# A gated-parallel backbone layer: the gate's sum and the query and key transposes placed later in TensorE's order

## The chip, the cores and the metric

The kernel runs on one core of a Trainium2 chip. The metric is the device time of one execution in microseconds (us), and the figure that counts is the median of several executions. Engines are named as the profile names them: PE is TensorE's matmul side and PEld its weight loads, DVE is VectorE, ACT is ScalarE, POOL is GpSimd, SP is the engine that issues the DMA transfers.

## The reference

The layer takes 1024 latent tokens and 256 context tokens of width 1024. Cut to what bears on the change:

```python
mod_x = silu(c) @ w_ada + b_ada              # shift, scale and gate of width 1024 each
sh_x, sc_x, g_x = split(mod_x, 3)
pl = project(modulate(x, sh_x, sc_x), w_in)  # one input projection, split in eleven parts
pc = project(modulate(ctx, sh_c, sc_c), w_in)
...                                          # (A) gated linear attention, both directions
q1, q2, k1, k2, dv = diff_streams(pl[5], pl[6], pl[7], diff_q_norm, diff_k_norm)
                                             # per head: t * rsqrt(mean(t^2) + eps) * gain
q1, q2, k1, k2 = apply_rope(...)             # latent tokens only
o_diff = diff_attention(q1, q2, [ck1, k1], [ck2, k2], [cv, dv], lam)   # (B)
out_x = combine(...)                         # gates, two branch projections, one output projection
x = x + g_x * out_x
```

Two things in it are touched. The gate `g_x` is the last third of `mod_x`: a vector of 1024 numbers, each a sum over 1024 products, which the kernel wants on all 128 partitions. The queries and keys of branch (B) are normalised per group of 64, rotated, and then needed transposed, with the head's channels on the partitions.

## The kernel before

**Stages.** A start (to some 80 us) makes the modulation and the normalised inputs, transposed. Then the input projection streams its weights in column blocks of 512: keys and queries of branch (A), a gate part, three parts as a seven-product block scheme (`pairs`, about 215 to 485 us), and from about 480 us the list `late` of `phase_a`: keys of branch (B) in two column halves (`dk`, 10 token tiles each), a gate part (`gg`), queries of branch (B) in two halves (`dq`, 8 token tiles each), and one block of a merge gate. Alongside these late jobs the four heads of the gated linear attention run (`gla_head`). Differential attention follows (about 910 to 1440 us), with the rest of the projections as filler, and the output projection ends the kernel. Products are made from a high and a low part of each float32 operand, three matmuls for one.

**The order is planned when the program is written.** The four compute engines are scheduled by hand (`manual_schedule`), so every engine runs its instructions in the order in which they are emitted, and only semaphores make it wait. The order of emission comes from a discrete-event planner, the class `Driver`. The tasks are Python generators. What a task yields is the time at which it wants to go on. `Driver.now` is the planned time of TensorE; `Driver.op` adds a cost for each instruction to the planned time of its engine and notes when each tile will be ready (`ready`). `At(t)` lets a task go on up to 1 us ahead of `t` (`AHEAD`), `AtPE(t)` not before TensorE's planned time has reached `t`:

```python
def _at(self, at, prio, gen):
    t = at
    t = max(t, self.now) if isinstance(t, AtPE) else max(t - self.AHEAD, self.now)
```

`when(x)` gives the planned time at which tile x is ready as `At`, `whenpe(x)` the same as `AtPE`. While a task waits for its time, the planner emits whatever other task is due, those of the lowest `prio` first; the projection's stream of matmuls has `prio` 9 and takes what is left. DMA issues are emitted by the same tasks onto SP's queue, in the same order; a `store` goes out when its source is planned to be ready. Buffers are counted: `acq(tag)` makes a task wait until a buffer of that tag is free in the plan, `rel(tag, e)` frees it at the planned time `e`. The tags that matter here: `raw` (3 buffers for weights as loaded), `w` (18), `p` (5), `pl` (4), `mm` (3 banks for projection results), `tp` (2 banks for transposes).

**The gate's sum.** `job_gate` (line 745) works through the 1024 gate columns in two halves. For each half it loads `w_ada` in four pieces into `raw`, and VectorE multiplies each of eight row blocks by its conditioning column and adds it into `gb`. Then one matmul of `gb` with a matrix of ones (`self.ones`) sums over the partitions into a `tp` bank (the trace shows it as two matmul records of tp<-gb,ones). VectorE adds the bias, GpSimd halves the result into `gb`, and behind both halves `gb` is stored to `d_gb`. `to_gla`, which exchanges buffers before the gated linear attention, waits for that store; the values are used in the output projection.

**Queries and keys.** `post_qk` (line 1312) runs once for each of the 20 + 16 tiles of `dk` and `dq`. It takes two `p` buffers, squares the projection result on ScalarE (p<-mm), applies gain and rotation on VectorE, sums the squares per group, and lets GpSimd form the power -0.5 (sm<-sm,nhalf) and scale the tile (p<-p,sm). Then TensorE transposes the tile in four blocks of 128 into a `tp` bank (tp<-ident,p), the two `p` buffers are released, ScalarE and VectorE split the result into two `pl` buffers, and two stores write them to `d_kT` or `d_qT`.

In the trace all matmuls have line 335 and all transposes line 361, because they are issued by the helpers `mm` and `tr`; instructions of ACT, DVE and POOL have line 197. They are told apart by the tiles' names.

Of the kernel before, what the change touches and what calls it, by code (L numbers as in the profile page):

```python
# [228 lines left out]
class Hybrid:  # L229
# [515 lines left out]
    def job_gate(self):  # L745


        a = self.a
        yield from self.acq("gb")
        gb = self.t("gb", [P, 2, 512])  # L750
        for n in range(2):
            o = 2048 + n * 512
            for kk in range(NK // 2):
                yield from self.acq("raw")
                raw = self.t("raw", [P, 2, 512])
                self.dma(raw, a["w_ada"][0][kk * 256:(kk + 1) * 256, o:o + 512].rearrange("(k p) c -> p k c", p=P))
                yield self.d.when(raw)
                for j in range(2):
                    k = 2 * kk + j
                    c = self.col[:, k:k + 1]  # L760
                    if k == 0:
                        e = self.dve.tensor_scalar(gb[:, n], raw[:, j], c, None, ALU.mult)
                    else:
                        e = self.dve.scalar_tensor_tensor(gb[:, n], raw[:, j], c, gb[:, n], ALU.mult, ALU.add)
                    yield e
                self.rel("raw", e)
            yield from self.acq("p")
            bias = self.t("p", [P, 512])
            self.dma(bias, a["b_ada"][0:1, o:o + 512].to_broadcast([P, 512]))
            yield self.d.whenpe(gb)  # L770
            yield from self.acq("tp")
            pm = self.t("tp", [P, 512])
            e = self.mm(pm, self.ones, gb[:, n], True, True)
            yield e
            yield self.d.when(bias)
            e = self.dve.tensor_tensor(bias, pm, bias, ALU.add)
            self.rel("tp", e)
            yield e
            self.rel("p", self.pool.tensor_scalar(gb[:, n], bias, 0.5, 0.0, ALU.mult, ALU.add))
        self.store([(self.d_gb, gb)], ("gb", 1), ev=self.ev_gb)  # L780
# [531 lines left out]
    def post_qk(self, isk, c, i, pm):  # L1312

        nc = self.nc
        g8 = lambda ap: ap.unsqueeze(1).to_broadcast([P, 8, 64])
        pv = pm.rearrange("p (g e) -> p g e", e=64)
        if isk and (c, i) == (1, 9):
            self.rel("hc", self.d.now, 16)
        yield self.ev_rope[isk]
        yield from self.acq("p", 2)  # L1320
        sq = self.t("p", [P, 8, 64])
        self.act.activation(sq, pv, AF.Square)
        ss = self.t("sm", [P, 8])
        r = self.t("p", [P, 8, 64])
        if i >= 8:
            e = self.dve.tensor_tensor(r, pv, g8(self.gains[:, isk, 0]), ALU.mult)
        else:
            e = self.dve.tensor_tensor(r, pv, g8(self.rope[:, 0, i]), ALU.mult)
        yield self.d.when(sq)
        self.dve.tensor_reduce(ss, sq, AX.X, ALU.add)  # L1330
        if i < 8:
            rv = sq.rearrange("p g (a h e) -> p g a h e", a=2, h=2)
            xv = pv.rearrange("p g (a h e) -> p g a h e", a=2, h=2)
            sv = self.rope[:, 1, i].rearrange("p (a h e) -> p a h e", a=2, h=2)
            for hh in range(2):
                e = self.dve.tensor_tensor(rv[:, :, :, hh], xv[:, :, :, 1 - hh],
                                           sv[:, :, hh].unsqueeze(1).to_broadcast([P, 8, 2, 16]), ALU.mult)
            self.dve.tensor_tensor(r, r, sq, ALU.add)
            if (c, i) == (1, 7):
                self.rel("rope", self.d.when(r))  # L1340
        self.rel("mm", e)
        yield self.d.when(ss)
        self.pool.tensor_scalar(ss, ss, 1.0 / 64, EPS, ALU.mult, ALU.add)
        self.pool.tensor_tensor(ss, ss, self.nhalf, ALU.pow)
        yield self.d.when(r)
        e = self.pool.tensor_tensor(r, r, ss.unsqueeze(2).to_broadcast([P, 8, 64]), ALU.mult)
        yield AtPE(e)
        yield from self.acq("tp")
        yield from self.acq("pl", 2)
        pt = self.t("tp", [P, 4, P])  # L1350
        rf = r.rearrange("p g e -> p (g e)")
        for j in range(4):
            e = self.tr(pt[:, j], rf[:, j * P:(j + 1) * P])
        self.rel("p", e, 2)
        yield e
        hi = self.t("pl", [P, 4, P], F32R)
        lo = self.t("pl", [P, 4, P], F32R)
        e = yield from self.split(pt, hi, lo)
        self.rel("tp", e)
        o = self.tok(i) if isk else i * P  # L1360
        dst = [self.d_kT[j][c] if isk else self.d_qT[c][:, :, j] for j in range(2)]
        self.store([(dst[j][:, :, o:o + P].rearrange("h p t -> p h t"), x) for j, x in enumerate((hi, lo))],
                   ("pl", 2), ev=self.ev_st["dk" if isk else "dq", c, i])
# [1131 lines left out]
```

## Time and profile before

| | us |
|---|---|
| median of 3 executions | 1676.13 |
| lowest and highest | 1675.11, 1677.49 |
| the profiled execution | 1676.87 |
| its span, first to last instruction | 1675.2 |

Busy shares of the span: PE 98%, PEld 81%, DVE 70%, ACT 48%, POOL 36%. A window line gives a stretch of the span, its length, the busy time of each engine in it with the number of instructions, the granted TensorE clock as a part of full speed, the share of the DMA engines and the rate. A timeline line gives start, duration, engine, line and operation, with the tiles written and read, and in brackets the idle time of the engine before it and what ended that. The duration of a group of matmuls includes the tail of its last one, which overlaps the next group.

### The profile page before, as it was taken

What the parts mean: (1) busy time and instruction counts of PE and PEld (TensorE: products, weight loads), DVE (VectorE), ACT (ScalarE), POOL (GpSimd) and SP (SyncE); (2) the same over time, 40 slices, a digit from 0 to 9 for tenths busy, and PEclk for the clock granted to TensorE, in tenths of its full rate; (3) what the DMA queues carried; (4) which work ended last, traced back from release to release, by engine and by line L of the source; (5) the groups of instructions that cost most, each with busy time, mean ns of one, the idle gap of its engine ahead of it and who ended that gap; (6) DMA issues with size and microseconds to landing.
All of it is one profiled execution on the core that took longest, in us unless ns stands there. A gap on an engine that the chain in (4) does not pass through costs nothing.

```text
span 1675.2 us, 24268 instructions
## 1 busy us (share of the span) xinstructions
PE 1634.8 (98%) x8389; PEld 1354.1 (81%) x8389; DVE 1166.3 (70%) x2019; ACT 796.3 (48%) x1640; POOL 606.4 (36%) x649
## 2 busy tenths in 40 slices
PE   7999999999999999999999999999999999999999
PEld 3688788888788888888878887888888888888887
DVE  4797853455578697687762878877887787438594
ACT  4766423343434535455441666665666556413141
POOL 1500200000156575464540544546565565700000
PEclk9999999999999999999999999999999999999999
DMA  8557947677573675646466244334336743277422
GB/s 304 175 204 259 326 163 248 230 276 276 201 251 120 187 218 174 186 137 177 123 187 162 68 122 129 106 107 133 114 107 196 247 126 108 65 255 250 158 78 76
DMA packets 248971, 294.44 MB, mean 176 GB/s; under 512 B 20712, under 2 KB 169104, under 8 KB 248848
## 3 DMA queue, kind: packets, MB, share of 16 engines
q1 hardware_dynamic: 248848, 292.90, 55.4%
q8 instruction: 66, 1.08, 0.3%
q14 instruction: 57, 0.47, 0.1%
HBM read 199.51 MB, written 93.32 MB: 175 GB/s over the span
## 4 chain that ended last, share of the span: by engine, by line
PE 43%; DVE 7%; ACT 3%; issue 2%; POOL 1%; DMA 1%; SPq 0%; ACTq 0%; DVEq 0%; POOLq 0%
PE mc L335 11%; PE mm L335 7%; PE mb L335 7%; PE s L335 6%; PE b L335 5%; DVE sm L197 4%; PE b L361 3%; ACT e L197 2%; DVE e L197 2%; PE go L335 1%; POOL at L197 1%; PE mz L335 1%; PE gs L335 1%; PE tp L361 1%; PE gt L335 1%
## 5 line engine op out<-in xcount | busy, mean ns | idle before, releaser
L335 PE MATMUL mm<-w,h 128*128 128x512 f32 x1260 | 319.1, 402 | 0.6 <-DVE w L197 0.4
L335 PEld LDWEIGHTS mm<-w,h 128*128 128x128 f32 x1260 | 231.9, 189 | 47.9 <-issue 1.0
L197 DVE TENSOR_REDUCE sm<-s 128x1 f32<-128x1024 f32 (+1 forms) x192 | 194.1, 1038 | 44.5 <-PE s L335 38.8
L335 PE MATMUL mb<-h,wt 128*128 128x512 f32 x744 | 202.0, 404 | 0.8 <-ACT ft L197 0.5
L197 ACT ACTIVATE e<-s,sm 128x1280 f32<-128x1280 f32 x128 | 170.1, 1333 | 60.8 <-DVE sm L197 50.0
L197 POOL TENSOR_TENSOR at<-ac,at 128x512 fp32r<-128x512 f32 x128 | 191.2, 1493 | 10.7
L197 POOL TENSOR_SCALAR at<-ac 128x512 fp32r<-128x512 f32 x128 | 101.3, 791 | 251.4 <-ACT ac L197 153.7
L335 PE MATMUL s<-hk,aq 128*128 128x512 f32 (+1 forms) x768 | 179.5, 366 | 6.1 <-ACT e L197 4.2
L335 PEld LDWEIGHTS mb<-h,wt 128*128 128x128 f32 x744 | 130.9, 189 | 24.4 <-ACT ft L197 2.2
L335 PEld LDWEIGHTS s<-hk,aq 128*128 128x128 f32 x768 | 120.5, 189 | 27.2 <-ACT e L197 11.7
L335 PE MATMUL mm<-h,w 128*128 128x512 f32 x576 | 137.6, 394 | 2.2 <-DVE h L197 1.1
L335 PE MATMUL mc<-h,wt 128*128 128x512 f32 x600 | 137.7, 390 | 0.0
L335 PE MATMUL b<-at,vv 128*128 128x256 f32 x960 | 131.3, 285 | 0.5 <-POOL at L197 0.3
L335 PEld LDWEIGHTS mc<-h,wt 128*128 128x128 f32 x600 | 112.1, 188 | 23.1
L335 PEld LDWEIGHTS mm<-h,w 128*128 128x128 f32 x576 | 106.9, 188 | 26.2 <-DVE h L197 1.6
L335 PEld LDWEIGHTS b<-at,vv 128*128 128x128 f32 x960 | 123.3, 190 | 5.7 <-POOL at L197 0.9
L197 DVE TENSOR_TENSOR w<-raw,w 128x512 fp32r<-128x512 f32 x120 | 92.6, 790 | 32.1 <-ACT w L197 30.9
L197 ACT ACTIVATE ac<-b 128x512 f32<-128x512 f32 x120 | 71.1, 601 | 90.9 <-PE b L361 84.2
L197 POOL TENSOR_TENSOR sm<-sm,nhalf 128x2 f32<-128x2 f32 (+2 forms) x94 | 102.3, 1089 | 26.0 <-DVE sm L197 20.8
L197 DVE SCALAR_TENSOR_TENSOR e<-e,sm,e 128x1280 f32<-128x1280 f32 x64 | 110.4, 1725 | 1.0
L197 ACT ACTIVATE w<-raw 128x512 fp32r<-128x512 f32 x120 | 72.5, 629 | 70.8 <-DVE raw L197 22.8
L197 POOL TENSOR_TENSOR p<-p,gdif 128x512 f32<-128x512 f32 x12 | 16.2, 1359 | 242.6 <-DMA d_dv<-pl 194.6
(283 smaller groups left out, 2914.2 us busy)
## 6 DMA issues: line engine op xcount, KB each, us to landing
raw<-in_w_in SPq DMA_DIRECT2D x63, 512.0 KB, 4.5
g<-d_s SPq DMA_DIRECT2D x32, 640.0 KB, 5.0
aq<-d_qT SPq DMA_DIRECT2D x128, 128.0 KB, 3.1
d_dv<-pl SPq DMA_DIRECT2D x40, 256.0 KB, 2.1
gv<-d_v SPq DMA_DIRECT2D x40, 256.0 KB, 3.1
d_kT<-pl SPq DMA_DIRECT2D x40, 256.0 KB, 2.9
hk<-d_kT SPq DMA_DIRECT2D x32, 320.0 KB, 4.9
vv<-d_dv SPq DMA_DIRECT2D x16, 640.0 KB, 5.7
```

The source lines that it names most:

```text
L197: self.ins = f(out, *args, **kw).ins
L335: self.ins = self.nc.tensor.matmul(out, lhsT, rhs, start=start, stop=stop, skip_group_check=more).ins
L361: self.nc.tensor.transpose(out, src, self.ident[:n, :n])
```

## The change

Two lines are changed, both times at which a task asks the planner to go on.

```diff
@@ job_gate
-            yield self.d.whenpe(gb)
+            yield AtPE(self.d.when(gb) + 4)
             yield from self.acq("tp")
             pm = self.t("tp", [P, 512])
             e = self.mm(pm, self.ones, gb[:, n], True, True)
@@ post_qk
         e = self.pool.tensor_tensor(r, r, ss.unsqueeze(2).to_broadcast([P, 8, 64]), ALU.mult)
-        yield AtPE(e)
+        yield AtPE(e + 1.5)
         yield from self.acq("tp")
         yield from self.acq("pl", 2)
```

In `job_gate` the matmul with the ones is emitted when TensorE's planned time is 4 us past the planned end of `gb`, where it was emitted at that end; this happens once in each of the two halves. In `post_qk` the four transposes are emitted when TensorE's planned time is 1.5 us past the planned end of the tile's scaling on GpSimd; this happens 36 times. The instructions themselves, their number, shapes and operands stay as they are. Everything that a task emits behind these points moves with them, and the planner may place the instructions of all later tasks differently.

## The prediction

> **What bounds the kernel now.** I read the busy shares of the page first, then the mean granted clock, then TensorE's waits over the whole span (columns: in total, times, longest).
>
> ```profile
> span 1675.2 us, 24268 instructions
> PE 1634.8 (98%) x8389; PEld 1354.1 (81%) x8389; DVE 1166.3 (70%) x2019; ACT 796.3 (48%) x1640; POOL 606.4 (36%) x649
> ...
> core 0: 1675.2 us, clock 0.998
> ...
> PE tp L361 <- DVE p L197: 5.0, 1, 5.0
> PE s L335 <- ACT e L197: 4.2, 9, 1.2
> ...
> PE tp L335 <- DVE gb L197: 2.5, 1, 2.5
> ...
> PE tp L361 <- POOL p L197: 2.2, 1, 2.2
> ```
>
> TensorE is busy for 1634.8 of 1675.2 us. An edit that only moves instructions takes none of this work away; it can touch the 40.4 us of idle time and what follows from them. Two waits belong to the edited lines: the gate's sum (tp from gb and ones) waited once for VectorE, 2.5 us, and a transpose (tp from p) waited once for GpSimd, 2.2 us. How these stand in their stretches I took from the busy time by window (window, length, busy time and count of PE, PEld, DVE, ACT, POOL, granted clock, DMA share, GB/s) and from the grouped line of the transposes between 480 and 880 us:
>
> ```profile
> 480.00:880.00 400.00, 397.21 (x2021) 334.82 (x2020) 303.27 (x557) 190.55 (x510) 223.44 (x279) 1.00 0.59 175
> 915.00:1440.00 525.00, 510.41 (x3069) 434.64 (x3069) 420.22 (x788) 317.66 (x647) 293.68 (x266) 1.00 0.44 127
> L361 PE MATMUL tp<-ident,p 128*128 128x128 f32 x144 | 21.7, 273 | 2.2 <-POOL p L197 2.2
> ```
>
> The 144 are 36 query and key tiles with four transposes each, and one tile of the 36 waits. (The 5.0 us at the head of the list lies ahead of 480 us, in the constants.) TensorE is idle for 400.00 - 397.21 = 2.79 us there, nearly all of it this one wait. The timeline shows both stalls with their neighbours:
>
> ```profile
> 171.47 22.62 PE L335 MATMUL mm<-w,h 128*128 128x512 f32 x99
> 193.72 1.43 DVE L197 SCALAR_TENSOR_TENSOR gb<-raw,col,gb 128x512 f32<-128x512 f32 x1 [0.25 <-DMA raw<-in_w_ada]
> 195.81 0.74 DVE L197 SCALAR_TENSOR_TENSOR gb<-raw,col,gb 128x512 f32<-128x512 f32 x1
> 196.60 2.08 PE L335 MATMUL tp<-gb,ones 128*128 128x512 f32 x2 [2.50 <-DVE gb L197]
> ...
> 860.14 1.64 POOL L197 TENSOR_TENSOR sm<-sm,nhalf 128x8 f32<-128x8 f32 x1
> 861.56 0.94 PE L335 MATMUL mm<-h,w 128*128 128x512 f32 x3
> 862.46 1.22 POOL L197 TENSOR_SCALAR_AFFINE_SELECT gsc<-gsc 128x256 f32<-128x256 f32 x2 [0.68 <-ACT gsc L197]
> 863.65 1.04 POOL L197 TENSOR_TENSOR p<-p,sm 128x512 f32<-128x512 f32 x1
> 864.75 0.67 PE L361 MATMUL tp<-ident,p 128*128 128x128 f32 x4 [2.24 <-POOL p L197]
> 865.16 0.41 DVE L197 TENSOR_TENSOR gsc<-gsc 128x256 f32<-128x256 f32 x1
> 868.87 0.59 PE L335 MATMUL go<-gsf,gqe 128*128 128x256 f32 x2
> 869.30 0.59 PE L335 MATMUL go<-gsb,gqe 128*128 128x256 f32 x2
> 870.16 0.60 PE L361 MATMUL tp<-ident,p 128*128 128x128 f32 x4
> ```
>
> In the first stall TensorE stands from 194.10 to 196.60 until VectorE's last product into gb ends at 196.55; that chain waited for a load. In the second it stands from 862.51 to 864.75: GpSimd scales the tile only after its two masks on gsc, and ends at 864.69. Behind each stall the clock drops, which two windows show:
>
> ```profile
> 196.25:199.66 3.41, 3.06 (x5) 1.83 (x6) 3.31 (x5) 2.34 (x4) 1.70 (x1) 0.50 0.91 275
> 865.26:868.67 3.41, 3.41 (x11) 2.69 (x10) 1.01 (x2) 0.60 (x1) 2.77 (x3) 0.50 0.95 244
> ```
>
> Twice the granted clock is 0.50 for 3.41 us. A mean of 0.998 leaves 0.002 x 1675.2 / 0.50 = 6.7 us at half speed in the whole span, so these 6.82 us are practically all of it. TensorE works for 3.06 and 3.41 us in them at half rate and so loses 1.53 and 1.71 us. The stalls cost 2.50 + 1.53 = 4.03 and 2.24 + 1.71 = 3.95 us, 7.98 together.
>
> **The change, part by part.** It adds and removes no instruction and no byte. The program writes its order against a planned clock; the change lets the gate's sum enter TensorE's order 4 planned us behind gb (two times), and each tile's four transposes 1.5 us behind the scaling (36 times). With 22.62 / 99 = 0.2285 us for a matmul in the stream, this is room for about 17 and 6 matmuls ahead of the moved ones, where the planner has them.
>
> Gate. The lateness was 2.50 us, the room is 4, so the stall goes and its half clock with it: -4.03 us. The bounds are -4.03, and 0 if the loads come later by as much as the sum was moved. What was queued behind the waiting sum is the stream of input projection matmuls; they now run ahead of it. Moved along are the bias addition on VectorE, the scaling on GpSimd, the store of d_gb on SP, and after the first sum the whole second half of the loop: its raw loads, its eight products and its sum, 8 us late in all at the end.
>
> ```profile
> 151.07 1.02 PE L335 MATMUL tp<-gb,ones 128*128 128x512 f32 x2
> ...
> 196.57 0.38 SPq L300 DMA_DIRECT2D raw<-in_w_in  x1
> ...
> 202.53 0.32 SPq L300 DMA_DIRECT2D d_gb<-gb  x1
> ...
> 208.57 0.64 ACT L197 ACTIVATE w<-raw 128x512 fp32r<-128x512 f32 x1 [0.72 <-PE mm L335]
> ...
> 216.76 2.88 PE L335 MATMUL tp<-w,h 128*128 128x512 f32 x12
> raw<-in_w_in SPq DMA_DIRECT2D x63, 512.0 KB, 4.5
> ```
>
> The first sum (151.07) waits for nothing now, so its delay earns nothing. The load that takes over a raw buffer from the gate starts at 196.57, lands at about 201 by the median of 4.5 us, and is converted from 208.57 on, for matmuls that start at 216.76: 7 us of slack to the conversion and more behind it. The second half starts 4 us later, so I price this at nothing; if the slack were gone, each us of lateness would be a us of idle TensorE at 216.76. d_gb (202.53) is needed for the change of buffers behind 480 us.
>
> Query and key transposes. GpSimd was 2.24 us late, the room is 1.5. What is late next is the masked score gsc: VectorE adds its halves until 865.57, and a third of the go matmuls need it. From 862.51 TensorE has three mm (0.69), the two pairs of go that don't need gsc (0.43 each, from 868.87 to 869.30) and the four transposes (0.36): 1.91 us of work in 3.06, whatever their order, which leaves 1.15 us idle. The bounds are 0 (the planner finds more matmuls for this place) and 2.24 (none). Whether 1.15 us lowers the clock: the nine waits for ACT e reach 1.2 us, lie behind 915 us, and the granted clock of that window is 1.00. So I take no half clock: -3.95 + 1.15 = -2.80 us.
>
> [...]
>
> The other 35 tiles wait for nothing and gain nothing. What they issue comes 1.5 us later: ACT's copy and VectorE's remainder into pl, two stores on SP, and the release of two p buffers and one tp. The last of them are the nearest to a consumer:
>
> ```profile
> 866.08 6.44 SPq L300 DMA_DIRECT2D d_qT<-pl  x4
> 873.68 0.66 SPq L300 DMA_DIRECT2D aq<-d_qT  x1
> 876.45 32.94 PE L335 MATMUL mm<-h,w 128*128 128x512 f32 x144
> 910.12 2.13 PE L335 MATMUL s<-hk,aq 128*128 128x512 f32 x10 [0.74 <-ACT p L197]
> ```
>
> The loads of the queries stand behind these stores on SP (873.68), but the first scores come at 910.12, behind 32.94 us of matmuls that cover the 1.5 us. Without that cover the start of attention would be 1.5 us late once.
>
> Sum against the profiled execution, 1676.87 us outside its span of 1675.2: 1676.87 - 4.03 - 2.80 = 1670.0. The median of the runs is 1676.13, 0.74 lower, so 1669.3.
>
> **The rivals.** *One of the stalls stays.* If gb's load is later by 4 us too, or the tile's place still leaves 2.24 us idle and a half clock. For it: the DMA share is 0.91 and 0.95 in the two windows, and 1.5 is less than 2.24. Only the gate cured: 1676.13 - 4.03 = 1672.1; only the tile: 1673.3.
>
> *The gain is given back in attention.* Everything behind 150 us is planned anew, and the 915 to 1440 us stretch has 525.00 - 510.41 = 14.6 us idle in small waits. If the new order has half as much again there, 7.3 us, the time is 1676.6. Against it: the moved instructions end before 880 us and the 32.94 us of matmuls lie between, so attention starts from much the same state.
>
> *Slower: the p buffers.* A tile holds two of five p buffers from its square until its transposes are through.
>
> ```profile
> 730.93 0.60 PE L361 MATMUL tp<-ident,p 128*128 128x128 f32 x4
> 841.49 0.59 ACT L197 ACTIVATE p<-mm 128x512 f32<-128x512 f32 x1
> 850.09 0.60 PE L361 MATMUL tp<-ident,p 128*128 128x128 f32 x4
> ```
>
> The tile of 841.49 holds them for 850.69 - 841.49 = 9.2 us. Query tiles come every (870.16 - 730.93) / 15 = 9.3 us. If other users of p left room for one tile at a time, the hold would set the pace; at 10.7 us the 16 query tiles would cost 16 x 1.4 = 22 us, and the time is 1691. It decides from 6.8 / 16 = 0.43 us a tile. Against it: two tiles fit, and TensorE's 0.55 us of other idle time in 400 us show no such wait.
>
> *The change does nothing.* If the planner has nothing else to issue in the added room, the order stays: 1676.1. The stream of matmuls that surrounds both places speaks against it.
>
> **How the numbers follow.** About 0.2%, 3.4 us, can be told from no change: faster is below 1672.8, slower above 1679.5. Forecast 0.62; one stall stays 0.15; given back 0.11; p buffers 0.08; nothing 0.04. Faster has 0.60 of the forecast, 0.09 of the second case and 0.02 of the third: 0.71. Slower has the 0.08 and 0.04 of the third: 0.12. The rest, 0.17, is the same. The forecast alone runs from 1668.2 (no idle left at the tile) to 1670.4 (all 2.24 us left without a half clock), with an eighth of attention's 14.6 us to either side 1666.4 to 1672.2. The range takes a quarter of it below, 3.6 us, so 1664.6, and goes up to 1677.5, which holds the cases of one stall, nothing, and most of the third.
>
> **What would show it.** Right: the wait of tp for gb is gone, no window behind 190 us has a clock of 0.50, the wait of tp for POOL p is gone or below 1.5 us with some of it now at go, and TensorE's busy time falls by about the 3.2 us of the half clock. Wrong: a clock of 0.50 anywhere behind 20 us; waits of mm or tp for w at 216 us; a larger idle time than 14.6 us in attention; waits at p between 480 and 880 us.

## The result, and the profile after

The changed kernel takes 1667.39 us (median of 6 executions, 1666.21 to 1668.69) against 1676.31 us (median of 6, 1672.31 to 1677.49) before: 8.9 us less, a ratio of 0.995 with a 95% interval of 0.9937 to 0.9963. (The differences in this text are those of the medians; the ratios are on record beside them and differ from the quotient of the medians by up to 0.0005.) The profiled execution took 1668.69 us. Its page, mean clock and the head of TensorE's waits (total, times, longest):

```profile
span 1666.9 us, 24241 instructions
PE 1633.3 (98%) x8389; PEld 1353.9 (81%) x8389; DVE 1155.4 (69%) x2019; ACT 795.9 (48%) x1640; POOL 605.2 (36%) x649
...
core 0: 1666.9 us, clock 0.999
...
PE tp L361 <- DVE p L197: 5.1, 1, 5.1
PE s L335 <- ACT e L197: 3.9, 8, 1.2
```

Neither wait of the edited lines, tp for gb or tp for POOL p, is in the list any more. The windows of the changed kernel (columns as in the prediction):

```profile
62.79:66.20 3.41, 3.41 (x10) 2.64 (x9) 2.21 (x5) 2.99 (x11) 0.96 (x2) 0.50 0.60 228
194.00:202.00 8.00, 8.00 (x37) 6.63 (x36) 7.86 (x11) 2.58 (x5) 3.38 (x2) 1.00 0.73 244
480.00:880.00 400.00, 399.31 (x2038) 337.21 (x2037) 290.80 (x552) 187.87 (x506) 222.14 (x278) 1.00 0.58 173
915.00:1440.00 525.00, 510.74 (x3093) 436.41 (x3091) 416.27 (x788) 317.15 (x651) 301.26 (x274) 1.00 0.44 126
```

TensorE is busy without a break where the gate's sum stood, and idle for 0.69 us instead of 2.79 between 480 and 880 us. The clock is 1.00 in both. There is one half clock left, at 62.79 us, in a part whose order the change doesn't touch. Where the time went is read from the same instructions in both traces: a product of the decay (gs from l, the third in the trace), the first matmul of the pairs (tp from w, h) and the first score (s).

```profile
110.12 0.40 PE L335 MATMUL gs<-l,l 128*128 128x512 f32 x1
```

That is the kernel before, whose other two marks are in the prediction (216.76 and 910.12). The changed kernel:

```profile
111.96 0.40 PE L335 MATMUL gs<-l,l 128*128 128x512 f32 x1
...
214.29 2.88 PE L335 MATMUL tp<-w,h 128*128 128x512 f32 x12
...
903.06 2.60 PE L335 MATMUL s<-hk,aq 128*128 128x512 f32 x12 [0.69 <-ACT p L197]
```

It enters 1.84 us late; of this the half clock at 62.79 us can account for 3.41 / 2 = 1.71. From there to the pairs it gains 1.84 + 2.47 = 4.31 us (the gate), to the first score another 4.60 (the tiles), and to the end 1.15. The last is no gain of the change: TensorE's operations behind 890 us stand in the same order in all fourteen traces, and eleven of the twelve experiments below, whatever they change, show 0.9 to 1.4 there. So it is most likely a loss of the one profiled execution of before. The two places in the changed kernel's timeline:

```profile
198.51 0.74 DVE L197 SCALAR_TENSOR_TENSOR gb<-raw,col,gb 128x512 f32<-128x512 f32 x1
201.86 1.02 PE L335 MATMUL tp<-gb,ones 128*128 128x512 f32 x2
...
855.04 4.35 PE L335 MATMUL mm<-h,w 128*128 128x512 f32 x18
856.24 1.04 POOL L197 TENSOR_TENSOR p<-p,sm 128x512 f32<-128x512 f32 x1
857.24 1.22 POOL L197 TENSOR_SCALAR_AFFINE_SELECT gsc<-gsc 128x256 f32<-128x256 f32 x2
859.23 0.59 PE L335 MATMUL go<-gsf,gqe 128*128 128x256 f32 x2
861.82 0.60 PE L361 MATMUL tp<-ident,p 128*128 128x128 f32 x4
```

gb is ready at 199.25 and the sum starts at 201.86. The tile that was late is another matter: its transposes did not only move by 1.5 us. GpSimd now scales it (856.24) ahead of the masks, 18 matmuls of the projection (855.04) stand where there were six, three on either side of its transposes, and all twelve go matmuls come ahead of its transposes, which start 4.5 us behind the scaling.

### The profile page after: what moved, and what is told of

Read it like the earlier page. It is cut to its first block, busy times and chain, and to the rows that moved or that the text cites. A ratio compares the mean times of both kernels' runs of the same rounds, so it can differ in the third digit from the quotient of the medians.

```text
span 1666.9 us, 24241 instructions
## 1 busy us (share of the span) xinstructions
PE 1633.3 (98%) x8389; PEld 1353.9 (81%) x8389; DVE 1155.4 (69%) x2019; ACT 795.9 (48%) x1640; POOL 605.2 (36%) x649
## 4 chain that ended last, share of the span: by engine, by line
PE 80%; DVE 8%; ACT 4%; DMA 3%; issue 2%; POOL 2%; SPq 0%; ACTq 0%; DVEq 0%; POOLq 0%
PE mm L335 29%; PE mc L335 11%; PE mb L335 7%; PE s L335 6%; PE b L335 5%; PE tp L335 5%; DVE sm L197 4%; PE go L335 4%; PE gs L335 4%; PE gt L335 4%; PE b L361 3%; ACT e L197 2%; DVE e L197 2%; PE tp L361 2%; DMA raw<-in_w_in 1%
## 5 line engine op out<-in xcount | busy, mean ns | idle before, releaser
L197 DVE TENSOR_TENSOR w<-raw,w 128x512 fp32r<-128x512 f32 x120 | 85.8, 737 | 29.9 <-ACT w L197 28.9
```

Of the source, the lines that this page charges most:

```text
L197: self.ins = f(out, *args, **kw).ins
```

## The experiments

Each is an edit of the kernel before, except one. "Before" in each group was run on the same chip; its medians were 1675.51 us (e1 to e4), 1676.23 (the f runs and e6) and 1675.03 (e5, e7, e8, e9). The profiled executions are cut at the three marks; the numbers are what each takes in a stretch against the profile of before, in us, beside where its clock is halved (start of the stretch, of those behind 190 us and ahead of the end). Each halved stretch is 3.41 us long, that of e9_qk_075 6.83. The scatter of a single execution is seen where an edit changes nothing: the gate's stretch of the six kernels with the gate as before goes from -1.19 to +1.30.

| kernel | gate | tiles | rest | half clock at |
|---|---|---|---|---|
| changed kernel | -4.31 | -4.60 | -1.15 | none |
| e1_gate | -4.22 | -1.49 | -1.33 | none |
| e5_gate_second | -4.17 | -0.23 | -1.18 | 861.22 |
| e6_gate_second_1us | -2.73 | -2.35 | -0.93 | none |
| e8_gate_earlier | +3.62 | -0.43 | -1.20 | 200.27, 869.28 |
| e2_qk | +0.17 | -3.79 | -1.19 | 197.38 |
| e3_one_tile | +0.15 | +0.48 | -1.36 | 197.90, 866.91 |
| e4_other_tiles | -1.19 | -4.40 | -1.25 | none |
| f1_keys | +1.30 | -2.59 | -0.99 | 199.14 |
| f5_first_key_tile | +0.03 | -1.83 | -1.24 | 197.55 |
| f3_queries_second | +0.03 | -2.79 | -1.29 | 197.46 |
| e9_qk_075 | -4.37 | +6.40 | -1.23 | 652.33 |
| e7_double | -4.36 | +10.97 | -0.13 | 650.44, 875.72 |

**The two parts alone.**

```diff
-            yield self.d.whenpe(gb)
+            yield AtPE(self.d.when(gb) + 4)
```

> Only the gate's sum is moved by 4 us. Theory (a stall of 2.50 us and the half clock behind it go): 4.0 us faster than before, no half clock and no wait of tp for gb near 196 us, the tile's wait of 2.2 us near 865 us and its half clock still there. Rival (the stall alone counts, the half clock would have come anyway): 2.5 us faster. Rival (the gain of the whole change comes from the new order behind 480 us): no change.

1671.25 us, ratio 0.9971 (0.9959 to 0.9982): 4.3 us less, as the theory has it. The tile's wait is still there, but in the profiled execution without a half clock. Wait and clock of e1_gate:

```profile
PE tp L361 <- POOL p L197: 2.2, 1, 2.2
...
855.00:875.00 20.00, 17.77 (x93) 14.89 (x92) 11.23 (x20) 6.11 (x12) 8.20 (x10) 1.00 0.88 236
```

This is why e1_gate gains 1.49 us in the tiles' stretch, too: the half clock of before (1.71 us) did not come, at an unchanged wait. The order is no reason: TensorE's operations in e1_gate differ from those of before only between 150 and 206 us.

```diff
-        yield AtPE(e)
+        yield AtPE(e + 1.5)
```

> Only the query and key transposes are moved by 1.5 us. Theory: the tile's wait of 2.24 us and its half clock go, the gate's stay, and with e1_gate the two sum to the whole change: 4.0 to 4.9 us faster than before (3.95 for stall and clock, up to 0.9 more by the aligned times of the changed kernel); by the prediction's 1.15 us of remaining idle time 2.8. Rival (p buffers held longer cost something on every tile, and the gate pays for it): slower than before or less than 2 us faster.

1672.23 us, ratio 0.9978 (0.9969 to 0.9987): 3.3 us less, between the prediction's 2.8 and the 4.0 to 4.9 of the theory. The wait at the tile is gone. The parts sum to 4.3 + 3.3 = 7.6 of the 8.9 us; the interval of the whole change, 0.9937 to 0.9963, goes from 6.2 to 10.6 us and holds both.

**Which tiles make the gain.** First the late tile alone, then all others.

```diff
-        yield AtPE(e)
+        yield AtPE(e + (1.5 if (isk, c, i) == (0, 1, 6) else 0))
```

> Only the transposes of the one query tile that waited 2.24 us (second column half, tile 6) are moved by 1.5 us; the other 35 tiles and the gate are as before. In TensorE's order its four transposes then stand three matmuls later. Theory: those three matmuls fill 0.69 us, so 1.5 us of waiting stay; if the half clock needs more idle time than that, 2.4 us faster, if not 0.7 us faster. Rival (the gain is that of the other tiles' new order): no change.

1676.78 us, ratio 1.0003 (0.9994 to 1.0012): nothing. The timeline of e3_one_tile shows why:

```profile
865.11 1.04 POOL L197 TENSOR_TENSOR p<-p,sm 128x512 f32<-128x512 f32 x1
865.40 1.30 DVE L197 TENSOR_TENSOR w<-raw,w 128x512 fp32r<-128x512 f32 x1
866.75 0.68 PE L335 MATMUL mm<-h,w 128*128 128x512 f32 x1 [2.32 <-DVE w L197]
867.22 1.06 PE L361 MATMUL tp<-ident,p 128*128 128x128 f32 x4
```

TensorE's order differs from that of before only between 862 and 877 us here. The third of the three matmuls that were to fill the gap needs the low part of a weight that VectorE finishes at 866.70. The same operation stands in the trace of before, hidden by the tile's wait:

```profile
863.94 1.30 DVE L197 TENSOR_TENSOR w<-raw,w 128x512 fp32r<-128x512 f32 x1
```

It ends at 865.24 there, when GpSimd's scaling had been done for 0.5 us. So the tile was not late by itself; TensorE stood ahead of VectorE and GpSimd together, and the wait only changed its name.

```diff
-        yield AtPE(e)
+        yield AtPE(e + (0 if (isk, c, i) == (0, 1, 6) else 1.5))
```

> All query and key tiles but that one are moved by 1.5 us; the gate is as before. Theory (35 tiles had nothing to gain, the one that waited still meets its operand late): within 1.5 us of before, with a wait of some 2 us at that tile and a half clock. Rival (the new order of everything behind 490 us takes the late tile away, whichever tile is moved): 4 to 5 us faster, no wait of tp for POOL p over 1 us.

1671.68 us, ratio 0.9974 (0.9964 to 0.9983): 3.8 us less, without any room at the tile that was late. The theory has fallen and the rival holds, if a little under its 4 to 5 us. The next three ask how little is enough.

```diff
-        yield AtPE(e)
+        yield AtPE(e + (1.5 if isk else 0))                          # f1_keys
+        yield AtPE(e + (1.5 if (isk, c, i) == (1, 0, 0) else 0))     # f5_first_key_tile
+        yield AtPE(e + (1.5 if (isk, c) == (0, 1) and i != 6 else 0))  # f3_queries_second
```

> Only the 20 key tiles (some 490 to 655 us) are moved by 1.5 us, none of the query tiles, among them the one that waited 2.24 us near 865 us. Theory now (the late tile is an accident of the order in which its neighbours stand on TensorE, GpSimd and VectorE, and a changed order further ahead shuffles it away): wait and half clock near 865 us gone, 4 to 4.6 us faster at that place. Rival (the moved tiles must be near the late one, the query tiles): the wait stays, no change.

> One single tile, the first key tile (transposed at 496 us), is moved by 1.5 us. The planner orders everything behind it anew. Theory of the accident: the wait near 865 us may go or stay, or another appear; where it goes, 4 to 4.6 us faster, with the room of 1.5 us at the other tiles playing no part. Rival (the room at the 35 or 36 tiles is what helps): the wait of 2 us stays and the time is that of before within 1.5 us. Planned neighbours of the late tile look as before (GpSimd masks gsc ahead of scaling the tile), so I expect the wait to stay at 1 to 2.5 us.

> Only the seven other tiles of the second query half (730 to 870 us, tile 6 itself not) are moved by 1.5 us. Theory of the accident: GpSimd's order at the late tile changes (the mask of gsc no longer between its power and its scaling), the wait goes, 4 to 4.6 us faster at that place. Rival (the gain needs the keys' new order): no change, wait of 2 us still there.

1673.62, 1673.50 and 1673.42 us, all with a ratio of 0.9984 (0.9974 to 0.9994, 0.9974 to 0.9993, 0.9975 to 0.9993): 2.6 to 2.8 us less each, less than the 4 to 4.6 expected at the place. The wait near 865 us and its half clock are gone in all three, but smaller new waits stand elsewhere: 1.01 us for ge at 603 us in f5_first_key_tile, 0.50 and 0.72 us for weights at 865 us in f3_queries_second. One tile moved by 1.5 us, 370 us ahead of the late one, does as much as twenty. In f1_keys and f3_queries_second GpSimd's mask no longer stands between the tile's power and its scaling, as expected for f3_queries_second (whose tiles are transposed between 808 and 871 us in the traces; at 730 us stands the first half). For f5_first_key_tile I had expected the wait to stay. There the mask still stands between, at 866.05 us, and yet 21 matmuls now cover the place; of all waits of tp for GpSimd it has only:

```profile
PE tp L361 <- POOL p L197: 0.3, 1, 0.3
```

**How safe a new order is.** The changed kernel with 0.75 in place of 1.5, and with both distances doubled.

```diff
-        yield AtPE(e + 1.5)
+        yield AtPE(e + 0.75)
```

> The gate as in the changed kernel, the transposes moved by 0.75 us, half as far. Theory of the accident (any new order of the tiles ahead takes the late tile away): as fast as the changed kernel within 1.5 us, no wait of tp for POOL p over 1 us. Rival (the 1.5 us of room matter, 2.24 us of lateness less 0.75): a wait of about 1.5 us stays at the tile, 1.5 to 3 us slower than the changed kernel.

1680.20 us, ratio to before 1.0036 (1.0023 to 1.0048): slower than before, although the gate's gain is in it. Both theories missed. Two new stalls stand in e9_qk_075:

```profile
647.43 1.22 POOL L197 TENSOR_TENSOR ge<-gk,ge 128x256 f32<-128x256 f32 x1
648.61 1.22 POOL L197 TENSOR_TENSOR p<-p,sm 128x512 f32<-128x512 f32 x1
649.88 0.66 PE L361 MATMUL tp<-ident,p 128*128 128x128 f32 x4 [2.49 <-POOL p L197]
...
810.79 0.73 PE L335 MATMUL mm<-w,h 128*128 128x512 f32 x2 [2.67 <-DVE w L197]
```

The first is a key tile that waited for nothing before: GpSimd serves the linear attention (ge) between the tile's power and its scaling. The half clock behind it lasts 6.83 us and costs 3.41. The second is a weight that VectorE splits too late.

```diff
-            yield self.d.whenpe(gb)
+            yield AtPE(self.d.when(gb) + 8)
-        yield AtPE(e)
+        yield AtPE(e + 3)
```

> Both distances are doubled: 8 us for the gate's sums, 3 us for the transposes. Theory (a later place costs nothing as long as buffers and loads have slack, and the order behind 490 us is drawn anew): as fast as the changed kernel within 2 us, 7 to 10 us faster than before, no wait of tp for gb. Rival (p, pl and tp buffers held longer, weights of the pairs loaded later): over 3 us slower than the changed kernel, with waits of mm or tp for w behind 210 us or for p behind 490 us.

1683.30 us, ratio 1.0051 (1.0036 to 1.0066): 8.3 us slower than before. The gate's stretch is as good as with 4 us; all of the loss is in the tiles' stretch. TensorE's waits there, 480 to 915 us of e7_double:

```profile
PE mm L335 <- DVE w L197: 5.4, 2, 3.6
PE gt L361 <- POOL ge L197: 3.6, 5, 1.1
```

No wait for p, pl or tp among the large ones: the rival of slower is right in sign, and the waits for w are there (646 and 872 us), but nothing shows the buffers as the cause. They are not excluded either: a buffer that runs out in the plan makes a task wait there, and would show in the trace as another order and not as a wait for it.

**The gate's room by doses.** Only the second sum by 4 us, only the second by 1 us, both sums up to 1 us earlier:

```diff
-            yield self.d.whenpe(gb)
+            yield AtPE(self.d.when(gb) + (4 if n else 0))   # e5_gate_second
+            yield AtPE(self.d.when(gb) + (1 if n else 0))   # e6_gate_second_1us
+            yield self.d.when(gb)                           # e8_gate_earlier
```

> Only the second of the gate's two sums is moved by 4 us; the first, which waited for nothing, is as before. Theory (the first sum's delay earns nothing): as fast as with both sums moved, 4.0 us faster than before, no wait of tp for gb, the tile's wait of 2.2 us near 865 us still there. Rival (the first sum's delay is needed, since it makes the loads of the second half later or earlier): less than 2 us faster.

> Only the second of the gate's two sums is moved, by 1 us where the whole change gives 4. Theory (the lateness was 2.50 us and the room is taken off it one for one): a wait of 1.5 us of tp for gb stays; 1.0 us faster if the half clock stays, 2.7 us if it goes with the shorter wait. Rival (the gain of the first sum's move or of the later loads): no change, the wait stays at 2.5 us.

> The gate's two sums are let into TensorE's order up to 1 us ahead of the planned end of gb, so they stand about six matmuls earlier than before. Theory (lateness is paid one for one): the wait of tp for gb at the second sum grows from 2.5 to about 3.8 us, with a half clock behind it, 1.0 to 1.4 us slower than before. Rival (the wait is set by something that moves with the sum): still 2.5 us and no change.

e5_gate_second: 1671.27 us, ratio 0.9977 (0.9966 to 0.9987), 3.8 us less; the first sum's move is worth nothing that can be told. e6_gate_second_1us: 1672.89 us, ratio 0.9985 (0.9976 to 0.9995), 3.3 us less, more than the 2.7 expected at most; part of it is the tile's half clock, which did not come in its profiled execution. Its sum and the clock around it:

```profile
199.25 1.12 PE L335 MATMUL tp<-gb,ones 128*128 128x512 f32 x2 [1.15 <-DVE gb L197]
...
196.00:204.00 8.00, 6.85 (x29) 5.00 (x28) 7.29 (x9) 3.23 (x6) 3.06 (x2) 1.00 0.84 287
```

The sum stands six matmuls later, and 2.50 - 6 x 0.2285 = 1.13 us of wait is what is left: lateness against room, one for one. e8_gate_earlier: 1679.71 us, ratio 1.0030 (1.0019 to 1.0042), 4.7 us slower, against the 1.0 to 1.4 expected. Six matmuls earlier, the longest wait grows from 2.5 to 4.2 us, 0.3 more than 2.50 + 6 x 0.2285 = 3.87:

```profile
PE tp L335 <- DVE gb L197: 4.9, 2, 4.2
```

The first sum, which waited for nothing, now waits 0.7 us as well. The gate's stretch of this profile is 3.62 us longer; the rest of the 4.7 is not traced to a place.

## Why the prediction was right, and where it was not

*What bounds the kernel.* Right: TensorE's busy time fell by 1.5 us only, and everything else came out of idle time. Of the 3.2 us forecast for the busy time, 3.24 us went with the two half clocks and 1.71 came with the one at 62.79 us. By its own list a clock of 0.50 anywhere behind 20 us was a sign of being wrong; that sign was too strict, since this one lies ahead of everything that the change moves.

*Gate, -4.03 us.* Right in mechanism and size: 4.3 us alone by the medians, 4.2 to 4.4 in the profiles with 4 us or more of room. e6 shows the lateness paid one for one; in e8 it costs somewhat more than that. The 1.53 us of half clock in the sum were those of one execution: e4_other_tiles has the same wait of 2.50 us without them. That the first sum earns nothing holds (e5), and so does the slack of the loads: no kernel with a moved gate shows a wait at the first pairs.

*Tiles, -2.80 us.* The sign was right, the mechanism wrong. The step that failed is "TensorE has three mm (0.69), the two pairs of go ... and the four transposes: 1.91 us of work in 3.06, whatever their order, which leaves 1.15 us idle". It took the neighbours as fixed and asked what 1.5 us of room would buy at this tile. In e3 it bought nothing, since the third of the three mm needed a weight that was as late; I had not looked up when VectorE ends it. With the other tiles moved (e4), or one far away (f5), the whole neighbourhood is planned anew and the wait is gone without any room there. The size was missed for this reason: of the 1.15 us that were to stay idle none is left at the tile, and the tiles gave 3.3 us in e2 and 4.6 in the changed kernel's profile. That the sign came out was in part luck: by the same working a room of 0.75 or 3 us would have gained as well, and e9 and e7 took 1680.20 and 1683.30 us, slower than before and outside the stated range.

*"The other 35 tiles wait for nothing and gain nothing."* True of their own place, false of the time: their move is what made the gain, and in e9 and e7 a move of the same tiles by other distances cost 6.4 and 11.0 us in the same stretch.

*The rivals.* The prediction put the danger of a new order into attention, since everything behind 150 us would be planned anew. It lies between 480 and 880 us instead. Behind 890 us TensorE's order is that of before in every kernel here, and with the gate alone moved it is so from 206 us on; attention's idle time is 525.00 - 510.74 = 14.3 us after 14.6. No wait shows the p buffers deciding anything, not even at 3 us; whether they shaped the plan was not tested. Nothing run here beats the changed kernel.

## What to carry to other kernels

In a kernel whose order is planned, a wait of the busiest engine can be a disagreement between plan and chip, as the two here were. At the gate, where one operand was late and its neighbours were not, room was taken off the wait one for one (six matmuls of 0.2285 us brought 2.50 us down to 1.15 in e6_gate_second_1us), and even 8 us of room cost nothing there (-4.36 us in e7_double, -4.31 in the changed kernel). Where several engines are late together, look at what every instruction of the neighbourhood waits for; a gain there is one draw among many orders. The constant that gave 4.6 us in the tiles' stretch at 1.5 took 6.4 at 0.75, so each value has to be measured.

## What the runs showed of the hardware

The same wait did not always bring the half clock. e4_other_tiles has the gate's sum where before has it, waits as long, and keeps the full clock:

```profile
196.61 1.13 PE L335 MATMUL tp<-gb,ones 128*128 128x512 f32 x2 [2.50 <-DVE gb L197]
...
194.00:202.00 8.00, 5.50 (x23) 4.12 (x23) 7.49 (x9) 2.67 (x5) 2.77 (x3) 1.00 0.82 259
```

In before, the half clocks begin at 196.25 and 865.26, in e3_one_tile at 197.90 and 866.91, in e8_gate_earlier at 200.27 and 869.28: 669.01 us apart each time, which is 196 steps of 3.413 us, the length of a halved stretch in the trace of before. A third in before, at 1674.22 us near the end of the span, is 237 such steps behind the second; those of e7_double at 650.44 and 875.72 are 66 such steps apart. So in these four executions the starts lie on a grid of 3.413 us, whose position differs from one to the next. Where a halved stretch gives the grid, the share of the grid step ahead that TensorE was idle can be counted: 2.15 of 3.41 us at 196.25 and 2.24 at 865.26 in before and 1.79 at 62.79 in the changed kernel, halved; in e1_gate the tile's wait of 2.23 us ends at 861.20 and falls into two steps, 0.66 and 1.57 us, not halved; in e4_other_tiles, counted back from the half clock at its end, 1.71 and 0.79 us, not halved. So how the idle time falls into the steps counted here. Between 20 and 1660 us of the traces of before and of the changed kernel, those three are the steps with the most idle time; the next, 1.22 us from 46.06 us of before, brought no half clock. In between it went either way (1.67 us idle: halved at 875.72 us of e7_double, not in e6_gate_second_1us).

The idle time of the step ahead does not settle it alone. Near the start a step of f3_queries_second that begins at 23.38 us, idle for 1.24 us, brought a half clock, and one of e8_gate_earlier at 60.32 us, idle for 1.61 us, did not. And e9_qk_075 stays halved for a second step although TensorE was busy all through the first:

```profile
648.92:652.33 3.41, 1.37 (x7) 1.08 (x8) 3.38 (x9) 0.60 (x1) 3.24 (x4) 1.00 0.57 128
652.33:655.74 3.41, 3.41 (x17) 3.27 (x16) 3.41 (x6) 0.00 (x0) 2.05 (x2) 0.50 0.24 77
655.74:659.16 3.42, 3.42 (x13) 2.94 (x13) 1.89 (x4) 1.08 (x2) 0.77 (x2) 0.50 0.17 40
```

No run shows why. One half clock costs, by estimate, up to 3.41 / 2 = 1.71 us, so whether one comes can be part of why medians and single profiles differ by 1 to 2 us: of the 26 executions of before that were run beside e1 to e4, the one with a mean clock of 1.000 was the fastest, 1673.16 us, and the two with 0.996 took 1677.33 and 1677.66.
